# A scheduler's table of TensorE durations is replaced by traced ones, and its order offsets, holds and engine choices are newly drawn

## The chip, the cores and the metric

The kernel runs on 1 core of one Trainium2 chip. The metric is the device time of one execution in microseconds, the median of several runs. The engines have the profile's names: PE is TensorE (matmuls; PEld its weight loads), DVE is VectorE, ACT is ScalarE, POOL is GpSimd, SP is SyncE, which issues the transfers.

## The reference, cut to what matters

Two kinds of layer act on 256 tokens of width 1024, two layers of each. The first kind mixes with a sparse attention of three branches (compressed, selected, windowed) and a gated spatial product, then runs an FFN with a convolution over three tokens, then a gated embedding product (PLE). The second kind mixes with pooling, gated linear attention and latent attention, then runs a gated FFN. Everything is float32.

```python
def first_block(x, p, ...):
    for i in range(DEPTH):                       # 2
        z = rms_norm(h, pre_mix_g[i]) @ w_in[i]  # 1024 x 2328
        ...
        h = h + rms_norm(mix, post_mix_g[i])
        f = conv_ffn(rms_norm(h, pre_ffn_g[i]), w_up[i], conv_w[i], conv_b[i], w_down[i])
        h = h + rms_norm(f, post_ffn_g[i])
        gate = jax.nn.sigmoid(rms_norm(h, ple_norm_g[i]) @ w_ple_gate[i])
        h = h + gate * (p[i] @ w_ple_proj[i])

def conv_ffn(x, w_up, conv_w, conv_b, w_down):   # 1024 x 5632, 2816 x 1024
    ...
    g, up = jnp.split(hc, 2, axis=-1)
    return (jax.nn.silu(g) * up) @ w_down
```

The second kind has the same frame: a projection of 1024 x 5808, the mixers, an output projection, and an FFN with a gate and no convolution.

## The kernel before

**Tiling.** Tokens lie in two tiles of 128 (t = 0, 1). All large products are made from split operands: `split` (L965) loads a weight block of up to 128 x 1024 float32 into a buffer `raw`, casts it to float32r in `wh` (the high part) and subtracts that from the block into `wl` (the low part). Inputs are split in the same way: pairs of `x4` buffers (the instruction lists call them `x`) for the features, `ah` and `al` for the FFN's activations. A product then is three matmuls, high by high, high by low and low by high, added up in one PSUM bank. There are 7 buffers `raw`, 5 `wh` and 5 `wl`, and four PSUM pools of two banks: `pa`, `pb`, `upp` and `trp` (transposes).

**The FFN** (`ffn`, L1162) goes over 22 feature tiles of 128, two to a step. For each, `up_mm` multiplies two weight blocks by all 256 tokens into a bank of `upp` (48 matmuls of 256 columns); DVE multiplies the bank by the row scale (`z`, printed `u<-upp,u`), ACT and DVE do the convolution in the first kind of layer, ACT the silu, then a product `u<-u,u`, a cast into `ah` and a difference into `al`. `down_mm` (L1175) multiplies that by one block of the down weights into two banks of `pa` (t = 0) and two of `pb` (t = 1), 12 matmuls of 512 columns. The down products of the last four tiles are held back (`HELD`) and done first for t = 0, then for t = 1. `post_part` and `post_done` (L1090, L1101) then take the squares of the banks on ACT, two small operations on POOL, and update `h` (printed `c_h`) on DVE; the transposes of the new `h` on PE begin the next stage (`norm_fold`, L1070).

**What sets the order.** The program is first recorded, not emitted: each call on an engine makes an `Op` with its predecessors (`Recorder.add`, L202 and following). `schedule` (L364) then plays the operations through with a table of durations, `_cost` (L307): it always takes the engine that can start earliest and from its ready operations the one with the lowest `prio`, gives out buffers as they come free, and keeps the ports that DVE and POOL share apart (`_PORT`). `emit` (L517) writes the operations out in the resulting order; its call at L522 is therefore the line of nearly every instruction in the profile. Nothing of the plan is kept at run time but the order on each engine; the hardware waits on semaphores alone.

Three tables steer it, by phase (`m1` first mixer, `f1` first FFN and its middle and last steps `f1m` and `f1e`, `p1` PLE, `m2`, `f2`, `f2m`, `f2e` the same of the second kind, `s`, `c1`, `s2` set-up). `SHIFT` (L526) moves the `prio` of a group of operations (key: group and kind; kind 0 transfers, 1 weight splits, 2 the rest), `HOLD` (L645) adds to the time from which a group may start, and `ALT` (L703) lists operations that go to another engine (`_alternative`, L275): casts and copies between ACT and DVE, two-input operations and subtractions between DVE and POOL. A phase's entries hold for every layer that runs through it. The middle steps share one set, so that all of them have one pattern: seven in each layer for `f1m`.

Of the kernel before, what the change touches and what calls it, by code (L numbers as in the profile page):

```python
# [293 lines left out]
def _n(lz):  # L294
    return int(np.prod(lz.shape[1:]))
# [11 lines left out]
def _cost(eng, meth, args, kw, reads, writes):  # L307
# [6 lines left out]
    if eng == "tensor":  # L314
        if meth == "transpose":
            return 107.0, None
        rhs = args[2]
        c = _n(rhs)
        if rhs.dtype == F32:
            d = 2 * max(2 * c / 2.4, 107.0)  # L320
        elif rhs.dtype == F32R:
            d = c / 2.4 if c >= 256 else 4 * c / 2.4
        else:
            d = c / 2.4
        return d, None
# [191 lines left out]
def emit(nc, order):  # L517
    for op in order:
# [9 lines left out]
        (0, 0): 11, (0, 2): -701  # L528
    },
# [5 lines left out]
    },  # L535
# [5 lines left out]
    },  # L541
    "f1m": {
        (1, 0): -520, (1, 1): -3630, (1, 2): -723, (2, 0): -251, (2, 1): 188, (2, 2): -699
    },
# [11 lines left out]
    },  # L556
# [5 lines left out]
    },  # L562
    "f2m": {
        (1, 0): -676, (1, 1): -278, (1, 2): -631, (2, 1): -3, (2, 2): -666
    },
# [23 lines left out]
    },  # L589
# [1422 lines left out]
```

## Time and profile before

| | |
|---|---|
| median of 3 runs | 1585.4 us (1585.31 to 1591.89) |
| profiled execution, its span from first to last instruction | 1583.9 us |
| PE busy | 1562.3 us, 99% |
| PEld busy | 1358.9 us, 86% |
| DVE busy | 1083.7 us, 68% |
| ACT busy | 761.7 us, 48% |
| POOL busy | 492.3 us, 31% |
| read from HBM | 267.94 MB, 170 GB/s over the span |
| PE's share of the chain of waits | 96% |

The page gives no time of its own for the profiled execution but the span; the median of the runs is 1.5 us longer than it. The granted TensorE clock is 0.999 of full speed over the span. Matmuls are pipelined and their ends are modelled: two that follow each other at full rate overlap in the drawing, and the distance of their starts is what one of them costs. A wait that the profile lists is idle time in front of an instruction with the releaser that came last. An instruction list names buffers with numbers; in the profile's rows they are left out.

### The profile page before, as it was taken

To read this page: it belongs to the slowest core of one execution; us is meant where nothing else is said; L and a number is where in the kernel's file an instruction comes from. 1 tells how busy PE (TensorE), PEld (TensorE's weight loads), DVE (VectorE), ACT (ScalarE), POOL (GpSimd) and SP (SyncE) were. 2 spreads that over 40 slices of the span, in tenths; PEclk is the share of its full clock that TensorE was granted. 3 is DMA by queue.
4 is the path that set the end of the run, shared out by engine and by line. 5 is a ranking of instruction groups with operands and counts; after the bars stand their busy time and mean duration, and the time that the engine had idled before them with its cause. 6 is when DMAs were issued, how large, how long until landed. Compare 5 with 4: busy or idle time off the path is not lost.

```text
span 1583.9 us, 24617 instructions
## 1 busy us (share of the span) xinstructions
PE 1562.3 (99%) x9421; PEld 1358.9 (86%) x9421; DVE 1083.7 (68%) x1582; ACT 761.7 (48%) x1333; POOL 492.3 (31%) x428
## 2 busy tenths in 40 slices
PE   7999999999999999999999999999999999999998
PEld 6778999988778999988888888999988888889997
DVE  6777877888777877886645647566566455675664
ACT  4566555554666545556453444323354534343242
POOL 2433111122433111115233552323443326424233
PEclk9999999999999999999999999999999999999999
DMA  8643765745644656736534556566555344555571
GB/s 271 221 147 103 216 186 176 217 129 172 202 128 129 211 180 189 211 121 194 180 109 132 166 186 193 172 188 188 163 183 186 107 139 160 193 173 174 178 224 38
DMA packets 264091, 270.60 MB, mean 171 GB/s; under 512 B 11698, under 2 KB 196645, under 8 KB 263973
## 3 DMA queue, kind: packets, MB, share of 16 engines
q1 hardware_dynamic: 263972, 269.03, 55.0%
q8 instruction: 74, 1.21, 0.3%
q14 instruction: 45, 0.36, 0.1%
HBM read 267.94 MB, written 1.05 MB: 170 GB/s over the span
## 4 chain that ended last, share of the span: by engine, by line
PE 96%; DVE 2%; ACT 1%; DMA 1%; SPq 0%; issue 0%; POOL 0%; DVEq 0%; POOLq 0%; ACTq 0%
PE pa L522 36%; PE upp L522 35%; PE pb L522 19%; PE trp L522 5%; DMA raw<-in_w_in_dram 1%; DVE wl L522 1%; DVE u L522 1%; SPq L522 0%; ACT L522 0%; ACT u L522 0%; ACT junk L522 0%; DVE x L522 0%; DVE wh L522 0%; ACT x L522 0%; POOL sm L522 0%
## 5 line engine op out<-in xcount | busy, mean ns | idle before, releaser
L522 ACT CAST wh<-raw 128x1024 fp32r<-128x1024 f32 (+3 forms) x382 | 393.0, 1033 | 470.3 <-PE upp L522 234.1
L522 DVE TENSOR_TENSOR wl<-raw,wh 128x1024 fp32r<-128x1024 f32 (+3 forms) x402 | 500.5, 1257 | 119.2 <-ACT wh L522 114.5
L522 PE MATMUL upp<-x,wh 128*128 128x256 f32 x2560 | 479.3, 283 | 0.0
L522 PE MATMUL pa<-wh,x 128*128 128x512 f32 (+1 forms) x1280 | 425.9, 402 | 3.7 <-DVE x L522 2.0
L522 PEld LDWEIGHTS upp<-x,wh 128*128 128x128 f32 x2560 | 406.3, 191 | 6.2 <-ACT wh L522 0.3
L522 PE MATMUL upp<-x,wl 128*128 128x256 f32 x1280 | 361.3, 283 | 1.5 <-DVE wl L522 1.5
L522 POOL TENSOR_TENSOR wl<-raw,wh 128x1024 fp32r<-128x1024 f32 (+2 forms) x94 | 228.7, 2436 | 282.8 <-ACT wh L522 121.7
L522 PEld LDWEIGHTS pa<-wh,x 128*128 128x128 f32 x1280 | 236.7, 189 | 53.2 <-ACT u L522 2.6
L522 PE MATMUL pa<-wl,x 128*128 128x512 f32 (+1 forms) x640 | 251.9, 401 | 0.0
L522 PEld LDWEIGHTS upp<-x,wl 128*128 128x128 f32 x1280 | 244.6, 191 | 3.4 <-DVE wl L522 2.0
L522 POOL TENSOR_TENSOR u<-u,u 128x256 f32<-128x256 f32 (+4 forms) x98 | 109.3, 1117 | 328.0 <-ACT u L522 288.0
L522 DVE CAST wh<-raw 128x1024 fp32r<-128x1024 f32 (+3 forms) x114 | 89.3, 787 | 100.3 <-PE pa L522 38.7
L522 PE MATMUL pb<-wh,x 128*128 128x512 f32 (+2 forms) x496 | 157.4, 384 | 0.0
L522 PEld LDWEIGHTS pa<-wl,x 128*128 128x128 f32 x640 | 120.8, 189 | 21.4 <-DVE u L522 0.8
L522 DVE TENSOR_TENSOR u<-upp,u 128x512 f32<-128x512 f32 x80 | 55.2, 690 | 72.4 <-PE upp L522 71.6
L522 PEld LDWEIGHTS pb<-wh,x 128*128 128x128 f32 x496 | 90.4, 188 | 15.8 <-ACT wh L522 0.6
L522 PE MATMUL pb<-wl,x 128*128 128x512 f32 (+2 forms) x248 | 92.2, 381 | 0.0
L522 PE MATMUL trp<-c_ident,u 128*128 128x128 f32 (+4 forms) x415 | 79.5, 274 | 2.6 <-DMA u<-in_pre_mix_g_dram 1.9
L522 POOL TENSOR_TENSOR sm<-sm,c_nhalf 128x1 f32<-128x1 f32 (+1 forms) x60 | 47.9, 799 | 106.3 <-DVE sm L522 104.3
L522 DVE SCALAR_TENSOR_TENSOR u<-u,c_cols_conv_w,u 128x254 f32<-128x254 f32 (+1 forms) x176 | 73.5, 478 | 0.0
L522 ACT ACTIVATE u<-u 128x256 f32<-128x256 f32 (+1 forms) x100 | 44.5, 445 | 55.5 <-DVE u L522 49.6
L522 POOL TENSOR_TENSOR al<-u,ah 128x256 fp32r<-128x256 f32 x22 | 22.6, 1027 | 148.0 <-ACT ah L522 78.0
(209 smaller groups left out, 2092.3 us busy)
## 6 DMA issues: line engine op xcount, KB each, us to landing
raw<-in_w_in_dram SPq DMA_DIRECT2D x112, 512.0 KB, 4.0
raw<-in_w_up_dram SPq DMA_DIRECT2D x88, 512.0 KB, 4.2
raw<-in_w_ffn_gu_dram SPq DMA_DIRECT2D x88, 512.0 KB, 4.8
raw<-in_w_down_dram SPq DMA_DIRECT2D x44, 512.0 KB, 4.4
raw<-in_w_ffn_down_dram SPq DMA_DIRECT2D x44, 512.0 KB, 4.1
raw<-in_w_o_dram SPq DMA_DIRECT2D x32, 512.0 KB, 4.0
raw<-in_cmp_w_dram SPq DMA_DIRECT2D x16, 512.0 KB, 4.9
raw<-in_w_ple_gate_dram SPq DMA_DIRECT2D x16, 512.0 KB, 3.9
```

Of the source, the lines that this page charges most:

```text
L522: f(*args, **kw)
```

## The change

The duration table `_cost` gets new values for PE: a float32r matmul of 256 or more columns costs 10.8 ns more, a float32 matmul 2.5 ns more and, where it contracts over 64 rows or fewer, another 190; a transpose costs 106.5 instead of 107. `SHIFT`, `HOLD` and `ALT` are replaced throughout (some 900 numbers). Two comments are gone. Nothing else differs: the same operations are recorded with the same predecessors.

```diff
     if eng == "tensor":
         if meth == "transpose":
-            return 107.0, None
+            return 106.5, None
         rhs = args[2]
         c = _n(rhs)
         if rhs.dtype == F32:
-            d = 2 * max(2 * c / 2.4, 107.0)
+            d = 2 * max(2 * c / 2.4, 107.0) + 2.5
+            if rhs.shape[0] <= 64:
+                d += 190.0
         elif rhs.dtype == F32R:
-            d = c / 2.4 if c >= 256 else 4 * c / 2.4
+            d = c / 2.4 + 10.8 if c >= 256 else 4 * c / 2.4
         else:
             d = c / 2.4
         return d, None
...
 SHIFT = {
     "c1": {
-        (0, 0): 11, (0, 2): -701
+        (0, 0): 148, (0, 2): -137
     },
...
 ALT = {
...
     "f1m": {
-        62, 81, 142
+        66, 142, 143, 146, 147
     },
```

What this does to the lists is shown at three places.

**Place 1: DVE and POOL in the last middle steps of the second FFN (`f2`, `f2m`).** `raw` to `wh` is the cast, `raw,wh` to `wl` the subtraction. DVE and then POOL, before:

```order
L522 CAST wh3_68<-raw3_61 128x1024
L522 CAST wh0_65<-raw6_64 128x1024
L522 CAST wh4_69<-raw1_59 128x1024
L522 TENSOR_TENSOR wl3_73<-raw3_61,wh3_68 128x1024
L522 TENSOR_TENSOR wl4_74<-raw1_59,wh4_69 128x1024
L522 CAST wh2_67<-raw2_60 128x1024
```

```order
L522 TENSOR_TENSOR al1_117<-u22_106,ah1_112 128x256
L522 TENSOR_TENSOR wl1_71<-raw6_64,wh0_65 128x1024
L522 TENSOR_TENSOR u20_104<-u2_86,u5_89 128x256
L522 TENSOR_TENSOR wl4_74<-raw5_63,wh4_69 128x1024
L522 TENSOR_TENSOR al2_118<-u12_96,ah2_113 128x256
```

and with the change:

```order
L524 CAST wh2_67<-raw3_61 128x1024
L524 CAST wh4_69<-raw0_58 128x1024
L524 CAST wh3_68<-raw1_59 128x1024
L524 TENSOR_TENSOR u16_100<-upp0_227,u14_98 128x512
L524 TENSOR_TENSOR u0_84<-u24_108,u16_100 128x256
L524 TENSOR_TENSOR wl4_74<-raw2_60,wh1_66 128x1024
```

```order
L524 TENSOR_TENSOR u21_105<-u6_90,u8_92 128x256
L524 TENSOR_TENSOR wl3_73<-raw4_62,wh0_65 128x1024
L524 TENSOR_TENSOR wl1_71<-raw3_61,wh2_67 128x1024
L524 TENSOR_TENSOR al1_117<-u21_105,ah2_113 128x256
L524 TENSOR_TENSOR wl2_72<-raw0_58,wh4_69 128x1024
L524 TENSOR_TENSOR wl0_70<-raw1_59,wh3_68 128x1024
```

DVE's fifth row of before, the subtraction of the block that it had cast two rows earlier, is POOL's third row now (`wl1` from `raw3` and `wh2`), and so are the two subtractions after it; DVE keeps the three casts.

**Place 2: PE at the end of the first FFN, where the PLE begins.** `ah`, `al` are the held down products, `c_h` the transposes of the new `h`, and the last rows the first matmuls on the new `x`. Before:

```order
L522 MATMUL pb0_225<-wh4_69,ah1_112 128x512
L522 MATMUL pb1_226<-wh4_69,ah1_112 128x512
L522 MATMUL pb0_225<-wl1_71,ah1_112 128x512
L522 MATMUL trp0_229<-c_ident0_190,c_h0_191 128x128 x4
L522 MATMUL pb0_225<-wh4_69,al1_117 128x512
L522 MATMUL trp1_230<-c_ident0_190,c_h0_191 128x128 x4
L522 MATMUL pb1_226<-wl1_71,ah1_112 128x512
L522 MATMUL pb1_226<-wh4_69,al1_117 128x512
L522 MATMUL pa1_224<-wh0_65,x41_76 128x512
```

and with the change:

```order
L524 MATMUL pb0_225<-wh0_65,ah1_112 128x512
L524 MATMUL trp0_229<-c_ident0_190,c_h0_191 128x128 x4
L524 MATMUL pb0_225<-wl0_70,ah1_112 128x512
L524 MATMUL trp1_230<-c_ident0_190,c_h0_191 128x128 x4
L524 MATMUL pb0_225<-wh0_65,al1_117 128x512
L524 MATMUL pb1_226<-wh0_65,ah1_112 128x512
L524 MATMUL pb1_226<-wl0_70,ah1_112 128x512
L524 MATMUL pb1_226<-wh0_65,al1_117 128x512
L524 MATMUL pa0_223<-wh4_69,x40_75 128x512
```

Both groups of transposes stand two down matmuls earlier, so that five instead of three down matmuls lie between the first group and the first matmul on `x`. The six `pa` matmuls ahead of this stretch, whose banks `h` is made from, stand one place earlier than before.

**Place 3: POOL in the middle steps of the first FFN (`f1m`).** Two steps and a half, before:

```order
L522 TENSOR_TENSOR u19_103<-u0_84,u2_86 128x256
L522 TENSOR_TENSOR u5_89<-u13_97,u16_100 128x256
L522 TENSOR_TENSOR u20_104<-u11_95,u14_98 128x256
L522 TENSOR_TENSOR u9_93<-u3_87,u8_92 128x256
L522 TENSOR_TENSOR u7_91<-u15_99,u26_110 128x256
```

and with the change:

```order
L524 TENSOR_TENSOR u14_98<-u17_101,u1_85 128x256
L524 TENSOR_TENSOR wl4_74<-raw1_59,wh3_68 128x1024
L524 TENSOR_TENSOR u2_86<-u20_104,u25_109 128x256
L524 TENSOR_TENSOR wl0_70<-raw3_61,wh0_65 128x1024
L524 TENSOR_TENSOR u5_89<-u15_99,u11_95 128x256
```

POOL makes one product and one weight subtraction in each step now, where it made two products; DVE has the other product and, in place of the subtraction, a second weight cast and an activation cast that were ACT's.

## Rows read from the trace of the kernel before

**Rows 1.** The page, busy us (share of the span) and instructions, first line

```profile
PE 1562.3 (99%) x9421; PEld 1358.9 (86%) x9421; DVE 1083.7 (68%) x1582; ACT 761.7 (48%) x1333; POOL 492.3 (31%) x428
```

**Rows 2.** Timeline, first and last matmul: start us, us, engine, line, operation, out<-in

```profile
5.61 1.09 PE L522 MATMUL trp<-c_ident,c_h 128*128 128x128 f32 x4 [5.61 <-DMA c_h<-in_x_dram]
...
1577.07 0.39 PE L522 MATMUL pb<-wh,al 128*128 128x512 f32 x1
```

**Rows 3.** Waits of PE, the eight longest: us in total, times, longest us

```profile
PE trp L522 <- DMA c_h<-in_x_dram: 5.6, 1, 5.6
PE pa L522 <- DVE x L522: 2.0, 3, 0.8
PE trp L522 <- DMA u<-in_pre_mix_g_dram: 1.9, 1, 1.9
PE upp L522 <- DVE wl L522: 1.5, 2, 0.8
PE pa L522 <- ACT u L522: 1.3, 2, 0.6
PE trp L522 <- DVE x L522: 0.9, 1, 0.9
PE trp L522 <- DVE u L522: 0.5, 1, 0.5
PE upp L522 <- DVE x L522: 0.3, 2, 0.2
```

**Rows 4.** Timeline of PE near the end, two matmuls of 512 columns

```profile
1576.39 0.39 PE L522 MATMUL pb<-wh,al 128*128 128x512 f32 x1
...
1576.62 0.39 PE L522 MATMUL pb<-wh,ah 128*128 128x512 f32 x1
```

**Rows 5.** Timeline of POOL, DVE and PE, last f2 steps, both layers (last row the second)

```profile
1068.59 2.86 POOL L522 TENSOR_TENSOR wl<-raw,wh 128x1024 fp32r<-128x1024 f32 x1 [2.58 <-DVE wh L522]
...
1069.10 4.55 DVE L522 TENSOR_TENSOR wl<-raw,wh 128x1024 fp32r<-128x1024 f32 x2
...
1071.41 0.40 PE L522 MATMUL upp<-x,wh 128*128 128x256 f32 x2
1072.58 0.39 PE L522 MATMUL upp<-x,wl 128*128 128x256 f32 x1 [0.77 <-DVE wl L522]
...
1073.04 0.28 PE L522 MATMUL upp<-x,wl 128*128 128x256 f32 x1
1073.16 0.28 PE L522 MATMUL upp<-x,wh 128*128 128x256 f32 x1
...
1501.32 0.38 PE L522 MATMUL upp<-x,wl 128*128 128x256 f32 x1 [0.77 <-DVE wl L522]
```

**Rows 6.** Groups by form, 160 to 320 us: busy us, mean ns | idle before, releasers

```profile
L522 DVE TENSOR_TENSOR wl<-raw,wh 128x1024 fp32r<-128x1024 f32 x58 | 70.6, 1227 | 15.4 <-ACT wh L522 14.7
...
L522 DVE CAST wh<-raw 128x1024 fp32r<-128x1024 f32 x9 | 6.3, 695 | 9.1 <-PE pb L522 8.7 <-PE upp L522 0.4
...
L522 DVE TENSOR_TENSOR u<-u,u 128x256 f32<-128x256 f32 x2 | 0.8, 418 | 0.0
L522 DVE CAST ah<-u 128x256 fp32r<-128x256 f32 x2 | 0.6, 290 | 0.6 <-POOL u L522 0.6
...
L522 POOL TENSOR_TENSOR u<-u,u 128x256 f32<-128x256 f32 x17 | 19.5, 1146 | 121.5 <-ACT u L522 117.9 <-issue 3.5
```

**Rows 7.** Groups by form of POOL, 960 to 1120 us

```profile
L522 POOL TENSOR_TENSOR wl<-raw,wh 128x1024 fp32r<-128x1024 f32 x13 | 32.4, 2494 | 38.0 <-ACT wh L522 18.2 <-DVE wh L522 9.3 <-issue 7.2
```

**Rows 8.** Timeline at the seam from the first FFN to the PLE, first layer

```profile
339.33 1.42 DVE L522 SCALAR_TENSOR_TENSOR c_h<-u,sm,c_h 128x512 f32<-128x512 f32 x2 [0.36 <-POOL sm L522]
...
340.25 0.60 PE L522 MATMUL trp<-c_ident,c_h 128*128 128x128 f32 x4
...
342.73 0.47 PE L522 MATMUL pa<-wh,x 128*128 128x512 f32 x1 [0.75 <-DVE x L522]
```

**Rows 9.** One middle step, busy us (x) of PE, PEld, DVE, ACT, POOL; clock, DMA share, GB/s

```profile
204.51:221.57 17.06, 17.06 (x122) 16.01 (x122) 13.08 (x19) 8.66 (x13) 2.15 (x2) 1.00 0.62 184
```

More of the change, by code (lines that the diff above doesn't have):

```diff
@@ L527 @@
     "c1": {
-        (0, 0): 11, (0, 2): -701
+        (0, 0): 148, (0, 2): -137
     },
     "f1": {
[4 rows of a table removed]
[4 rows of a table added]
     },
     "f1e": {
[4 rows of a table removed]
[4 rows of a table added]
     },
     "f1m": {
-        (1, 0): -520, (1, 1): -3630, (1, 2): -723, (2, 0): -251, (2, 1): 188, (2, 2): -699
+        (1, 0): -1530, (1, 1): -914, (1, 2): -670, (2, 0): 5043, (2, 1): 1147, (2, 2): -717
     },
     "f2": {
[10 rows of a table removed]
[10 rows of a table added]
     },
     "f2e": {
[4 rows of a table removed]
[4 rows of a table added]
     },
     "f2m": {
-        (1, 0): -676, (1, 1): -278, (1, 2): -631, (2, 1): -3, (2, 2): -666
+        (1, 0): 3215, (1, 1): -118, (1, 2): 32, (2, 0): -366, (2, 1): -1515, (2, 2): -1484
     },
     "m1": {
[22 rows of a table removed]
[21 rows of a table added]
     },
     "m2": {
[39 rows of a table removed]
[38 rows of a table added]
     },
     "p1": {
[5 rows of a table removed]
[5 rows of a table added]
     },
     "s": {
-        (0, 0): 76, (0, 2): 156
+        (0, 0): 87
     },
     "s2": {
-        (0, 0): 185
+        (0, 0): -3032, (0, 2): 1944
     },
@@ L646 @@
     "c1": {
-        (0, 0): 974, (0, 2): 1486
+        (0, 2): 1903
     },
     "f1": {
-        (3, 1): 62, (5, 0): 106, (5, 2): 7, (6, 2): 1094, (9, 2): 18, (12, 2): 519, (14, 1): 1238
+        (0, 0): 89, (1, 0): 153, (3, 0): 723, (3, 1): 207, (3, 2): 5, (5, 0): 1696, (6, 0): 261, (6, 2): 782,
+        (12, 2): 4, (13, 0): 289
     },
     "f1e": {
-        (1, 0): 569, (1, 1): 203, (2, 1): 693, (3, 0): 782, (6, 0): 548, (10, 2): 7, (11, 2): 115, (12, 2): 256,
-        (14, 2): 270
-    },
-    "f1m": {
-        (1, 0): 1474, (1, 1): 252, (2, 1): 275
+        (2, 0): 182, (2, 1): 390, (4, 1): 477, (12, 2): 358
     },
     "f2": {
[4 rows of a table removed]
[4 rows of a table added]
     },
     "f2e": {
-        (1, 1): 953, (2, 1): 1454, (3, 1): 191, (4, 1): 75, (5, 1): 294
+        (6, 0): 841, (6, 1): 120
     },
     "f2m": {
-        (1, 0): 3995, (1, 1): 715, (2, 1): 268
+        (1, 1): 2200, (2, 0): 21
     },
     "m1": {
[8 rows of a table removed]
[7 rows of a table added]
     },
     "m2": {
[15 rows of a table removed]
[14 rows of a table added]
     },
     "p1": {
-        (3, 2): 15, (6, 2): 4, (8, 0): 580, (8, 1): 2246, (10, 0): 1337, (10, 1): 3584, (11, 2): 70, (12, 1):
-        386, (13, 0): 1023, (13, 2): 251, (15, 0): 2398, (15, 1): 1400, (18, 2): 643
+        (6, 2): 4, (7, 0): 976, (8, 1): 2446, (10, 1): 3650, (12, 1): 998, (12, 2): 354, (13, 2): 245, (14, 0):
+        667, (15, 0): 1949, (15, 1): 922, (18, 2): 639
+    },
+    "s2": {
+        (0, 2): 61
     },
@@ L703 @@
 ALT = {
+    "c1": {
+        10
+    },
     "f1": {
-        79, 137, 148, 149, 216, 217
+        42, 51, 57, 61, 76, 79, 137, 139, 149, 152, 216, 217, 218
     },
     "f1e": {
-        28, 62, 224, 302, 303, 306, 336, 371, 372, 439, 504
+        62, 81, 108, 143, 144, 146, 161, 162, 242, 303, 371, 439, 504
     },
     "f1m": {
-        62, 81, 142
+        66, 142, 143, 146, 147
     },
     "f2": {
-        17, 31, 32, 39, 53, 145, 167, 168, 170, 226, 228, 230, 238, 279, 307, 308, 311, 349, 350, 405, 424, 482,
-        483, 520, 575, 576, 580, 621, 622, 649, 654, 674, 747, 765, 792, 793, 821, 822, 824, 896, 940, 968, 969,
-        972, 973
[4 rows of a table added]
     },
     "f2e": {
-        56, 57, 76, 103, 132, 206, 278, 280, 286, 312, 340, 342, 374, 402, 403, 407
+        29, 56, 58, 75, 102, 103, 130, 132, 135, 204, 208, 223, 250, 251, 282, 285, 286, 312, 313, 340, 341,
+        342, 345, 347, 374
     },
     "f2m": {
-        1, 28, 57, 58, 76, 130, 131, 134
+        1, 2, 28, 29, 57, 58, 60, 61, 132
     },
     "m1": {
[4 rows of a table removed]
[4 rows of a table added]
     },
     "m2": {
[6 rows of a table removed]
[7 rows of a table added]
     },
     "p1": {
-        5, 16, 32, 35, 37
+        31, 35, 84, 142
     },
     "s": {
-        5, 6, 9, 11
+        9, 11, 27
     },
     "s2": {
-        7, 18, 19, 21, 27, 34, 35, 36, 43
+        17, 18, 33, 35, 43, 48
     },
```

251 rows, old and new, of tables (ALT, HOLD, SHIFT) are left out of this document.

## The prediction

> **What bounds the kernel now.** I read the busy table first. PE is busy for 1562.3 us of a span of 1583.9 [rows 1]; the other 21.6 us are the most that better order alone could show. The first and last matmul give two fixed pieces of it [rows 2]: nothing runs on PE before 5.61 us, and the last matmul starts at 1577.07 and is over 0.39 us later, 6.4 us before the end. That leaves 9.6 us of idle PE between 5.6 and 1577.5. Then PE's list of waits [rows 3]: the eight largest make 14.0 us; 5.6 is the lead-in, 1.9 the wait for the first gain vector at 8.6 us, and 6.5 us in eleven waits stand in the body. No engine, queue or transfer bounds the kernel but PE; DVE (68%), ACT (48%) and POOL (31%) only have to be in time.
>
> A busy PE hides a little more. Matmuls of 512 columns start 0.23 us apart while each is drawn 0.39 us long [rows 4], so a wait is shown about 0.16 us too short. Eleven of them hide 1.8 us. What order can win in the body is therefore 6.5 + 1.8 = **8.3 us**, 0.5% of the time.
>
> Durations come from the profiled execution. Its span is 1583.9; the median of the three runs is 1585.4, so I add 1.5 us to every sum.
>
> **The change, part by part.**
>
> *The PE table.* It enters the schedule alone. No duration in it is executed, so it costs nothing itself; what counts is the order that it yields, together with the new offsets and holds.
>
> *PE's work.* The order lists hold the same matmuls, in number and in shape, before and after (9063 rows of work on each side); nothing on PE is an engine choice. Cost 0. SP issues the same 583 transfers, its last four unchanged.
>
> *Head and tail.* Up to the first matmul on weights PE's rows are the same but for one transpose that no longer stands between two weight matmuls; the first transfers, up to the third block of w_in, are issued in the same order, and the end is the same chain (squares of the last pb banks on ACT, two small POOL operations, DVE, the store). Cost 0, hidden by nothing, but unchanged.
>
> *The last f2 steps (place 1).* Here the trace shows what a collision costs. Two weight subtractions of DVE took 4.55 us together while POOL ran one of its own for 2.86 [rows 5]; elsewhere one takes 70.6 / 58 = 1.22 on DVE [rows 6]. So DVE lost 4.55 - 2.44 = 2.1 us, and PE, whose two matmuls from 1071.41 on would have been followed 0.24 later, at 1071.65, went on at 1072.58: 0.93 lost, of which 0.77 is shown as a wait. The same stands at 1501.32 in the second layer. In the new order this subtraction is POOL's, behind DVE's cast of the same tile; between the last matmul on its weight buffer's old contents and the first that reads the difference PE has 27 matmuls of 256 columns and 17 of 512, at spacings of 0.12 and 0.23 us [rows 4, 5] 7.1 us. Against it stand a cast of 0.70, the POOL subtraction of 2.49 to 2.86 and one more of that length ahead of it [rows 5 to 7]: 6.4 us at worst. I take the wait as gone: 2 x 0.93 = **-1.9 us**. What is late next there is POOL, with four such subtractions near each other.
>
> *The seam from the first FFN to the PLE (place 2).* The first matmul on the new x waits 0.75 us for DVE [rows 8]. Between the first four transposes of h and that matmul PE has three matmuls and four transposes now and gets five and four: 2 x 0.23 = 0.45 us more cover. But the transposes themselves move up with the pa matmuls ahead of them by only one place, and they already start 0.2 us behind the half of c_h that they read (339.33 + 0.71, against 340.25) [rows 8]. So the second 0.23 turns into a wait in front of the transposes. I take one place: 0.23 in each of two layers, **-0.5 us**; the bounds are 0 and -0.9.
>
> *The middle steps of the first FFN (place 3).* There are 7 in each layer, 14 in all, each 17.06 us with PE busy throughout; DVE is busy for 13.08 and POOL for 2.2 [rows 9]. In each, DVE gives one weight subtraction to POOL (-1.22) and takes one weight cast (6.3 / 9 = +0.70), one product u (0.42) and the cast of an activation (0.6 / 2 = 0.30) [rows 6]: 13.3 us. POOL gives away a product (-1.15) and gets the subtraction (+2.49): 3.5 us. ACT is relieved of a weight cast and an activation cast. PE still needs 17.06, so the step costs **0**: the cover is DVE's 3.8 us of idle time in each. If that cover is gone, see the second rival. The weights that POOL makes there are those of the down product, and PE reads them 109 matmuls of 256 and 25 of 512 columns after their buffer comes free, 18.8 us.
>
> *Everything else.* Of the other engine choices (altogether 84 more weight casts and 40 fewer weight subtractions on DVE) the trace shows no row where PE ends up waiting for a longer time. The remaining waits of the body are 6.5 - 1.5 - 1.5 = 3.5 us in seven places, 4.6 with what they hide. All of them stand in mixer stages that are redrawn. Bounds: all gone, -4.6; as many new ones, +4.6. I take 0, since nearest to a redrawn order under the same rules is the order that the trace shows.
>
> Sum: 1583.9 - 1.9 - 0.5 = 1581.5 for the span, **1583.0 us** for the run.
>
> **A rule weighed against the trace.** The pair in [rows 5] shows DVE held for 2.1 of the 2.86 us that POOL's operation took, and POOL itself lengthened by 0.37 over its 2.49 [rows 5, 7]. The Trainium skill, "SBUF — State Buffer", section "Who interferes with whom", says that DVE and GpSimd arbitrate for one shared port pair and that the one that comes second "fully blocks"; by that rule moving a two-input operation from DVE to GpSimd buys nothing while the other is at work. By that rule a step's DVE is held for the whole 2.49, which makes 13.3 + 2.49 = 15.8 us of 17.06: the sum stays at 1583.0, unless what is held is what PE reads next. The trace bears the rule out as far as one pair can, and it speaks against place 3, where POOL had no weight subtraction until now; that case is the second rival.
>
> **The rivals.**
>
> *A, the waits of the body go.* For it: the old table planned a 256-column matmul at 109 ns, where the trace shows pairs 0.12 us apart [rows 5], so its plan and the run drift by a tenth in the FFNs, and the new one doesn't. Against it: DVE's and POOL's planned times are untouched, and a plan in which PE is too fast makes producers early, which is slack the new order loses. All 8.3 us gone gives 1583.9 - 8.3 + 1.5 = **1577.1 us**, 0.5% faster.
>
> *B, POOL holds DVE in the first FFN.* Each of the 14 middle steps now has a POOL subtraction of 2.49 us on a DVE that is busy for 13.3 of 17.06. One hold of 2.1 us fits into DVE's idle 3.8 as long as no operation that PE needs soon is behind it. It decides from the point where the held operation is the subtraction that PE reads next, as at 1069.10, or where the multiply that frees the upp bank queues behind it. Then each step loses what the f2 seam lost: 14 x 0.93 = 13.0 us, so 1583.0 + 13.0 = **1596.0 us**, 0.7% slower. For it: that exact row. Against it: the weights that POOL makes are due 18 us later, so POOL may be the one that waits. A whole 2.49 in each step would be 34.9 us and 1617.9.
>
> *C, the change does nothing to the time.* Every wait that goes comes back elsewhere: 1585.4. This is inside "within 0.5%", as is the forecast.
>
> **How the numbers follow.** 0.5% is 7.9 us, about what a measurement of this kernel can tell from no change; faster means below 1577.5 and slower above 1593.3. The forecast with C, and all between them: 0.53. A, or A with part of the start's 1.9 us as well: 0.27. B and like collisions in the mixers of the second block, where POOL has most of its subtractions: 0.20. The range reaches down to A with that 1.9 us and a little of the loading phase, 1574, and up to B and one further us, 1597; about one in ten lies beyond either end. The part that the likeliest case alone would take is 1579 to 1588.
>
> **What would show it.** In the profile after: PE's busy time still 1560 to 1564 and its first and last matmul where they are; no wait of "upp" for DVE's wl of 0.7 us near 1072 and 1501; the wait of pa for DVE x behind the FFN seam down to about 0.5; middle steps of 17.06 us with DVE near 13.3, POOL near 3.5. Steps of 18 us, or DVE subtractions of more than 3 us beside POOL's between 180 and 300 us, would be B. The forecast is wrong if PE's waits in the body sum to under 2 us or to over 12.

## The result and the profile after

| | before | with the change |
|---|---|---|
| median | 1585.4 us | 1600.1 us (1597.5 to 1601.8, 4 runs) |
| ratio to the kernel before, 95% interval | | 1.0084 [1.0065, 1.0103] |
| profiled execution, span | 1583.9 us | 1595.7 us |

The change made the kernel slower by 0.8%, and its median lies just above the range of the prediction (1574 to 1597); 1583.0 was forecast. The profiled execution is the shortest of the four, so the profile accounts for 11.8 us of the 14.7 between the medians.

The busy table, first line, answers to [rows 1]:

```profile
PE 1569.6 (98%) x9421; PEld 1364.5 (86%) x9421; DVE 1200.8 (75%) x1641; ACT 659.6 (41%) x1216; POOL 634.6 (40%) x486
```

DVE is busy for 117 us more and POOL for 142 more, ACT for 102 less. 84 casts of 0.7 us less 40 subtractions of 1.2 would give DVE some 10 us, so most of DVE's growth is operations that got longer. PE's waits, the longest (us in total, times, longest), answer to [rows 3]:

```profile
PE trp L524 <- DMA c_h<-in_x_dram: 5.6, 1, 5.6
PE trp L524 <- DVE c_h L524: 3.9, 2, 1.9
PE trp L524 <- DMA u<-in_mlp_out_g_dram: 3.9, 1, 3.9
PE pb L524 <- DVE wh L524: 2.6, 2, 1.3
PE trp L524 <- DMA u<-in_pre_mix_g_dram: 1.5, 1, 1.5
PE pa L524 <- POOL x L524: 0.6, 1, 0.6
PE pa L524 <- ACT x L524: 0.5, 2, 0.3
```

Three of these lines are new: 3.9 us for c_h and 2.6 us for a cast wh, each once in both layers of the second kind, and 3.9 us for a tile of gain vectors at the start. Gone are the 1.5 us for DVE's wl and the 2.0 us for DVE's x of [rows 3]. The timeline at the first of the new places, the end of the second kind's mixer (DVE, POOL and PE; start us, us, engine, operation):

```profile
958.59 3.58 DVE L524 SCALAR_TENSOR_TENSOR c_h<-u,sm,c_h 128x512 f32<-128x512 f32 x2 [0.39 <-POOL sm L524]
...
959.26 2.36 POOL L524 TENSOR_TENSOR wl<-raw,wh 128x1024 fp32r<-128x1024 f32 x1 [0.71 <-ACT wh L524]
...
959.40 0.66 PE L524 MATMUL trp<-c_ident,c_h 128*128 128x128 f32 x4
...
962.22 0.66 PE L524 MATMUL trp<-c_ident,c_h 128*128 128x128 f32 x4 [1.94 <-DVE c_h L524]
```

The second half by itself:

```profile
959.26 2.91 DVE L524 SCALAR_TENSOR_TENSOR c_h<-u,sm,c_h 128x512 f32<-128x512 f32 x1
```

The two halves of c_h take 3.58 us together; the same pair takes 1.42 in [rows 8]. POOL's weight subtraction and the second half both start at 959.26 in the trace, and the rows can't tell which came first; but POOL's operation takes 2.36 and ends at 961.62, and the second half takes 2.91 and ends at 962.17. PE's transposes of that half start 2.2 us later than PE's own pace would have it. 38 us earlier stands the other one:

```profile
920.75 2.38 POOL L524 TENSOR_TENSOR wl<-raw,wh 128x1024 fp32r<-128x1024 f32 x1
920.81 0.69 DVE L524 TENSOR_TENSOR u<-pb,sm 128x512 f32<-128x512 f32 x1 [1.25 <-POOL sm L524]
...
921.42 2.25 DVE L524 CAST wh<-raw 128x1024 fp32r<-128x1024 f32 x1
...
923.73 0.50 PE L524 MATMUL pb<-wh,x 128*128 128x512 f32 x1 [1.27 <-DVE wh L524]
```

Beside this POOL operation DVE's product that reads a PSUM bank (pb) takes its usual 0.69; the cast behind it, from SBUF to SBUF, takes 2.25 instead of 0.69. That cast was ACT's before the change. Both places come again 432 us later. By the distances of matmul starts the four cost 2 x (2.19 + 1.43) = 7.2 us.

At the start SP issues the last gain vector at 19.28 us (before: 15.84), and PE stops for it:

```profile
19.28 0.29 SPq L524 DMA_DIRECT2D u<-in_mlp_out_g_dram  x1
```

```profile
22.61 0.41 PE L524 MATMUL trp<-c_ident,u 104*128 104x104 f32 x1 [3.87 <-DMA u<-in_mlp_out_g_dram]
```

Behind two of the stops the clock is lower as well (stretches; PE, PEld, DVE, ACT, POOL busy us; clock, DMA share, GB/s):

```profile
22.61:28.70 6.09, 6.08 (x15) 4.83 (x16) 3.82 (x4) 4.04 (x4) 0.00 (x0) 0.51 0.96 327
...
962.22:966.20 3.98, 3.98 (x20) 3.34 (x21) 3.83 (x7) 3.18 (x6) 0.06 (x1) 1.00 0.42 132
...
1393.76:1397.60 3.84, 3.84 (x12) 3.22 (x13) 3.31 (x5) 2.45 (x5) 0.00 (x0) 0.56 0.43 137
```

Behind the 3.9 us in which PE stood still, and behind the second of the two c_h waits, the granted clock is near its lower level of 1.2 GHz over stretches of 6.1 and 3.8 us; a 512-column matmul then starts 0.43 us after the one before instead of 0.23. By the distances of the 512-column matmuls that is 2.8 us more at the start and 1.4 behind 1393.76. Behind the first c_h wait it stays at 2.4 GHz.

In all, the first 50 us go like this, before and with the change:

```profile
0.00:50.00 50.00, 41.63 (x211) 34.47 (x212) 36.08 (x68) 22.07 (x32) 11.10 (x18) 1.00 0.90 286
```

```profile
0.00:50.00 50.00, 38.08 (x184) 31.45 (x185) 31.14 (x52) 22.52 (x33) 14.87 (x22) 0.93 0.81 253
```

PE starts 184 matmuls in them instead of 211.

The middle steps of the first FFN answer to [rows 9]:

```profile
232.80:249.98 17.18, 17.18 (x122) 16.04 (x121) 14.30 (x21) 7.01 (x12) 4.28 (x3) 1.00 0.62 183
```

### The profile page after: what moved, and what is told of

The parts are those of the page before. It is cut to its first block, busy times and chain, and to the rows that moved or that the text cites. A ratio compares the mean times of both kernels' runs of the same rounds, so it can differ in the third digit from the quotient of the medians.

```text
span 1595.7 us, 24664 instructions
## 1 busy us (share of the span) xinstructions
PE 1569.6 (98%) x9421; PEld 1364.5 (86%) x9421; DVE 1200.8 (75%) x1641; ACT 659.6 (41%) x1216; POOL 634.6 (40%) x486
## 4 chain that ended last, share of the span: by engine, by line
PE 95%; DVE 1%; DMA 1%; ACT 1%; POOL 1%; issue 0%; SPq 0%; DVEq 0%; POOLq 0%; ACTq 0%
PE upp L524 35%; PE pa L524 35%; PE pb L524 19%; PE trp L524 5%; DVE c_h L524 1%; DMA raw<-in_cmp_w_dram 0%; POOL sm L524 0%; DVE u L524 0%; DVE wh L524 0%; ACT junk L524 0%; SPq L524 0%; DMA c_h<-in_x_dram 0%; POOL wl L524 0%; DMA u<-in_mlp_out_g_dram 0%; ACT x L524 0%
## 5 line engine op out<-in xcount | busy, mean ns | idle before, releaser
L524 DVE TENSOR_TENSOR wl<-raw,wh 128x1024 fp32r<-128x1024 f32 (+2 forms) x358 | 475.8, 1340 | 64.3 <-ACT wh L524 61.6
L524 ACT CAST wh<-raw 128x1024 fp32r<-128x1024 f32 (+4 forms) x306 | 310.0, 1021 | 415.7 <-PE upp L524 181.7
L524 POOL TENSOR_TENSOR wl<-raw,wh 128x1024 fp32r<-128x1024 f32 (+2 forms) x138 | 344.9, 2506 | 229.8 <-DVE wh L524 97.4
L524 PE MATMUL pa<-wh,x 128*128 128x512 f32 (+1 forms) x1280 | 433.0, 404 | 1.1 <-POOL x L524 0.6
L524 PE MATMUL upp<-x,wl 128*128 128x256 f32 x1280 | 354.1, 283 | 0.0
L524 DVE CAST wh<-raw 128x1024 fp32r<-128x1024 f32 (+2 forms) x190 | 187.0, 988 | 127.8 <-PE pa L524 46.0
L524 DVE SCALAR_TENSOR_TENSOR u<-u,c_cols_conv_w,u 128x255 f32<-128x255 f32 (+1 forms) x176 | 74.8, 475 | 6.9 <-ACT u L524 6.7
L524 POOL TENSOR_SCALAR sm<-sm 128x1 f32<-128x1 f32 (+2 forms) x40 | 16.8, 421 | 147.8 <-ACT junk L524 117.6
L524 ACT ACTIVATE u<-pa,sm 128x512 f32<-128x512 f32 (+2 forms) x62 | 41.4, 676 | 73.4 <-PE pa L524 73.4
L524 POOL TENSOR_TENSOR al<-u,ah 128x256 fp32r<-128x256 f32 x38 | 38.1, 1005 | 82.6 <-DVE ah L524 77.5
```

Of the source, the lines that this page charges most:

```text
L524: f(*args, **kw)
```

## The experiments

Every kernel was timed in five rounds beside the kernel before. Nine of the twelve hold one kind of edit: a POOL operation on one column makes a subtraction of POOL wait for a DVE operation. It is put into the finished list, so that no order on any engine changes:

```diff
+def _behind(order, late, early, mark):
+    for a, b in zip(_nth(order, late, "gpsimd"), _nth(order, early, "vector")):
+        src = b.args[0].bitcast(F32)
+        ...
+        tok.eng, tok.meth, tok.args, tok.kw = "gpsimd", "tensor_scalar", (mark, src, 1.0, None), {"op0": ALU.mult}
+        order.insert(order.index(a), tok)
```

**1. POOL behind DVE at the two places**, the second half of c_h and the cast.

```diff
+    _behind(order, ("f2", 39), ("m2", 1605), mark)
+    _behind(order, ("m2", 1424), ("m2", 1454), mark)
```

> The changed kernel with four small POOL operations more: ahead of the weight subtractions that start at 920.75 and 959.26 us (and at their twins in the second layer, 432 us later) POOL copies one column of the result of DVE's cast of 921.42 or of the second half of c_h, so that the subtraction starts behind DVE's operation instead of just ahead of it. All engine orders are otherwise the same. Port theory (POOL's subtraction holds DVE for its whole length, and PE waits for what DVE makes): PE's gaps of 2.2 us at 962 and 1394 and of 1.4 us at 924 and 1355 go, 7.2 us, and with them the nine matmuls at half clock behind 1394, 1.8 us: about 1591, the two halves of c_h together 1.4 us in both layers, the cast 0.7. Rival (PE is simply ahead of its operands there: the weights that POOL makes, or the transposes, come late anyhow): DVE's operations get short, but PE waits as long one operation later: 1599 to 1601.

1589.2 us, ratio 1.0014 [1.0003, 1.0025]: 10.9 us come back between the medians. The two profiled executions differ by 8.2 us (1595.7 and 1587.5), which is about what the four places and the clock behind one of them cost; the other 2.7 us of the medians no kept trace accounts for. The timeline at the c_h place (mark is the small operation), the second half of c_h by itself, and the cast:

```profile
957.06 1.41 DVE L549 SCALAR_TENSOR_TENSOR c_h<-u,sm,c_h 128x512 f32<-128x512 f32 x2 [0.39 <-POOL sm L549]
...
958.56 0.24 POOL L549 TENSOR_SCALAR mark<-c_h 128x1 f32<-128x1 f32 x1 [1.54 <-DVE c_h L549]
...
958.75 2.41 POOL L549 TENSOR_TENSOR wl<-raw,wh 128x1024 fp32r<-128x1024 f32 x1
```

```profile
957.73 0.75 DVE L549 SCALAR_TENSOR_TENSOR c_h<-u,sm,c_h 128x512 f32<-128x512 f32 x1
```

```profile
921.43 0.69 DVE L549 CAST wh<-raw 128x1024 fp32r<-128x1024 f32 x1
```

The pair takes 1.41, its second half 0.75 instead of 2.91, the cast 0.69, all four waits are gone, and no new one stands behind them. POOL's two subtractions start some 1 and 2 us later than they could, and PE's list has no wait for them. The rival falls. The wait for the gains stays, at 2.9 us.

**2. The gain transpose later, and both edits.** PE's transpose of the gains and its copy are set 18 matmuls later.

```diff
+    tr = _nth(order, ("s", 26), "tensor")[0]
+    _later(order, [tr] + _nth(order, ("s", 27), "vector"), pe[pe.index(tr) + 18])
```

> The changed kernel with one transpose of PE (of the tile of small gain vectors, which waits 3.87 us for its transfer at 22.61 us) and its copy on DVE set 18 matmuls later; nothing else moves. Theory (one transfer that the plan has early and that SP issues late stops PE, which has other work ready): the gap of 4.0 us goes and so do the thirteen matmuls at half clock behind it, 2.7 us: about 1593.4. Rival (the start is bound by the weight transfers: what PE would do next isn't there either): PE waits for a wh, wl or x instead, 1597 to 1600.

> Both edits of the two runs before this together. Theory: the gains add up, 1600.1 - 9.0 - 6.7 = 1584.4, level with the kernel before. Rival (waits that go come back elsewhere): above 1592.

1598.0 and 1589.9 us, ratios 1.0066 [1.0049, 1.0083] and 1.0013 [1.0003, 1.0023]. The intervals with and without the edit overlap, for the changed kernel and for that of experiment 1. The theory falls: the wait for the gains is gone, but PE stops at 27.96 us for the next thing (PE's waits, this edit alone):

```profile
PE pa L549 <- ACT wh L549: 2.8, 1, 2.8
```

That wh comes from a weight block that SP had issued behind the gains. What was open: which order at the start sets the time.

**3. One half of the change each.** The scheduler's PE durations put back under the new tables, and the new durations put under the old tables (the lines of `_cost` in the diff of the change, reversed or alone).

```diff
-            d = c / 2.4 + 10.8 if c >= 256 else 4 * c / 2.4
+            d = c / 2.4 if c >= 256 else 4 * c / 2.4
```

> The changed kernel with the durations of PE in the scheduler's table as they were before; offsets, holds and engine choices stay the new ones. Theory (single collisions of a newly drawn order, POOL's subtractions ahead of DVE's operations, cost the time; the table of durations moves them but doesn't remove them): the order is drawn again, collisions stand at other places, 1590 to 1612. Rival (the new durations make the plan run late against the chip, and that is what costs): near the kernel before, 1583 to 1589.

> The kernel before with the new durations of PE in the scheduler's table alone; offsets, holds and engine choices stay the old ones. Theory (the tables of offsets and holds fit only the durations that they were drawn with, so either half of the change alone spoils the order): clearly slower than both, 1620 to 1720. Rival (truer durations give a better or equal order by themselves): 1578 to 1590.

1702.4 and 1654.1 us, ratios 1.0728 [1.0707, 1.0748] and 1.0422 [1.0403, 1.0441]. The first was expected at 1590 to 1612 and is far worse; the second came as expected. Durations and tables belong together: with either half alone PE's waits are many and everywhere (the longest of the first kernel's):

```profile
PE trp L522 <- DVE c_h L522: 8.6, 5, 3.8
PE trp L522 <- DVE u L522: 6.6, 5, 3.4
PE upp L522 <- DVE wl L522: 6.1, 6, 2.1
```

So the 0.8% can't be divided between the durations and the tables; "the new durations cost it" and "the tables cost it" are both the wrong question.

**4. The same edit in the kernel before.** First POOL's subtraction of [rows 5] behind DVE's first one (the first line), then also a place in the first kind of layer.

```diff
+    _behind(order, ("f2", 973), ("f2", 941), mark)
+    _behind(order, ("m1", 188), ("m1", 360), mark)
```

> The kernel before with one small POOL operation more in each layer of the second kind: the weight subtraction of POOL at 1068.59 us waits for DVE's subtraction of 1069.10, as the plan has it. Theory (that is the 0.93 us that PE loses at 1072.58 and at 1501.32): both waits go, 1.9 us, 1584.6 where the kernel before has 1586.5. Rival (PE waits for the same weights anyhow, or for POOL's one operation later): no difference, and a wait of 0.7 us or more stays within 5 us of the place.

> The kernel before with the small POOL operation at 1068.59 us that took it to 1583.5, and a second such one in the first kind of layer: the weight subtraction of POOL at 382.71 us waits for DVE's small products that it held for 2.1 us, and behind which PE waited for x at 389.49. Theory (the same hold, one more place): that gap of 1.1 us goes in the second of the two layers, 1582.4. Rival (x is late for other reasons, or POOL's subtraction gets late): 1583.5 or a little more, with a wait near 389 that stays.

1583.5 us, ratio 0.9982 [0.9973, 0.9991], and 1582.5 us, ratio 0.9981 [0.9972, 0.9989]: the only kernels of the study that beat the one before. The pair of DVE that took 4.55 us in [rows 5], and the second place, before and with the edit:

```profile
1069.03 2.35 DVE L547 TENSOR_TENSOR wl<-raw,wh 128x1024 fp32r<-128x1024 f32 x2
```

```profile
382.71 3.32 POOL L522 TENSOR_TENSOR wl<-raw,wh 128x1024 fp32r<-128x1024 f32 x1 [4.82 <-DVE wh L522]
...
383.68 2.56 DVE L522 TENSOR_TENSOR u<-u,c_rope_tok 128x32 f32<-128x32 f32 x3
...
389.49 0.33 PE L522 MATMUL trp<-wh,x 128*60 128x256 f32 x1 [0.94 <-DVE x L522]
```

```profile
385.32 0.35 DVE L547 TENSOR_TENSOR u<-u,c_rope_tok 128x32 f32<-128x32 f32 x3
...
385.97 2.41 POOL L547 TENSOR_TENSOR wl<-raw,wh 128x1024 fp32r<-128x1024 f32 x1
...
390.02 0.28 PE L547 MATMUL trp<-wh,x 128*60 128x256 f32 x1
```

Three tiny products took 2.56 us beside POOL and 0.35 ahead of it, and PE's wait six us later is gone. That the second edit shortens the time isn't shown: the intervals of the two ratios overlap almost wholly, and the profiled executions have spans of 1581.8 and 1582.2 us; the second has 3.4 us at half clock from 105.4 us on, which the first has not.

**5. POOL behind DVE wherever the plan has it there.** Each long two-input operation of POOL that the plan starts within 0.3 us of the end of a DVE operation that it counts as using the shared port now waits for that operation.

```diff
+    for a in [x for x in order if x.eng == "gpsimd" and x.port == "pool_read" and x.dur > 800]:
+        e = [x for x in order if x.eng == "vector" and x.port in ("two", "wide") and x.start < a.start - 1e-6]
+        if not e or a.start - e[-1].end > 300.0 or e[-1].args[0].dtype not in (F32, F32R):
+            continue
```

> The changed kernel with 133 small POOL operations more: wherever the plan starts a long two-input operation of POOL within 0.3 us of the end of a DVE operation that uses the shared port, POOL now waits for that DVE operation. The time that DVE is held falls from 170 us to under 60. Theory (a hold costs only where PE reads next what DVE makes, which four of them did): as with the first four, 1588 to 1591. Rival (170 us of held DVE delays PE all over, in small gaps too): under 1584. If POOL's 133 operations make POOL late, above 1593.

1607.4 us, ratio 1.0126 [1.0111, 1.0141]: the third of the outcomes. DVE was held less, but by far less than expected (142 us; 163 with the four edits of experiment 1, 170 in the changed kernel, 62 in the kernel before: the sum, over DVE's operations beside one of POOL, of what each took beyond the fifth percentile of its form, where that is over 0.15 us). The likely reason is that the next DVE operation meets the delayed subtraction; it was not followed place by place. And now PE waits for POOL:

```profile
PE upp L549 <- POOL wl L549: 6.4, 8, 1.2
```

These eight waits are a third of the 18.5 us between the profiled executions of experiment 1 and of this one (1587.5 and 1606.0); the rest is not taken apart. Fewer holds did not make a faster kernel. In the changed kernel there are some 155 held operations, and four of them stand in front of PE's waits for DVE, 7.2 us.

**6. The start, three more orders.** All have the edit of experiment 1. The first has that of experiment 2 too, and two weight blocks ahead of others on SP's queue; the second puts two blocks (one of them issued among the gains) and two small weights behind the gains again, with the two blocks that PE needs next ahead of these; the third moves ACT's and DVE's operations on these blocks along.

```diff
+    blocks = [_nth(order, ("m1", k), "sync")[0] for k in (81, 128, 171, 277, 278, 145)]
+    _later(order, blocks, _nth(order, ("s", 25), "sync")[0])
+    _later(order, [_nth(order, ("m1", 129), "scalar")[0]], _nth(order, ("m1", 82), "scalar")[0])
+    _later(order, [_nth(order, ("m1", 146), "scalar")[0]], _nth(order, ("m1", 161), "scalar")[0])
+    _later(order, [_nth(order, ("m1", 130), "vector")[0]], _nth(order, ("m1", 83), "vector")[0])
```

The first two lines alone are the second kernel.

> The kernel with both edits, and on SP's queue two weight blocks of w_in that PE needs from 27 us on (they were issued at 19.6 to 20.5 us) set ahead of two blocks that it needs later. Theory (the order of the weight transfers sets the start, the late gain vectors only hid it): the 2.3 and 1.0 us that PE waits at 27 to 29 us for ACT's wh and DVE's wl go, and most of the matmuls at half clock behind them: the excess of the first 50 us falls from 10.6 to about 5.5 and the time from 1589.9 to about 1585. Rival (too few bytes have landed by then, whatever their order): PE waits as long for the next block, 1588 to 1591.

> The changed kernel with the four POOL operations that let its subtractions wait, and SP's queue alone changed at the start: one block of w_in and two small compression weights, which stood ahead of the constants and gain vectors (issued at 5.6 to 7.3 us), go behind them, and the two blocks that PE needs from 27 us on come first behind the gain vectors. PE's order is the changed kernel's own. Theory (each 512 KB block ahead of the constants and gain vectors brings them in some 1.4 us later, and PE, DVE and the blocks behind wait in turn; the kernel before had a block and two small weights fewer there): the gap of 3 to 4 us at 22.6 falls under 1 and the excess of the first 50 us from 11 to about 7: 1585. Rival (what PE does in the first 50 us in the new order needs more bytes early, in any order of transfers): a wait of the same size at another block, 1588 to 1591.

> As the run before with SP's queue changed at the start, and ACT's casts and DVE's subtraction of these blocks moved with them: ACT's queue took the block first that now lands last, so that its cast at 25.83 us waited 8.3 us and PE's block stood behind it. Now ACT casts the block that PE needs first, then the next, and the late one two places later. Theory (the start loses time because the order of SP, ACT and PE no longer fit to each other in time; blocks earlier in all three queues give it back): the wait of 5.2 us at 28.8 falls under 1.5, the excess of the first 50 us from 14 to 7 or 8, 1585 to 1586. Rival (what PE does in the first 50 us of the new order can't be fed faster): again a wait of 3 to 5 us at a later block, 1588 to 1592.

1591.2, 1591.5 and 1591.6 us; ratios 1.0025 [1.0014, 1.0036], 1.0033 [1.002, 1.0045] and 1.0031 [1.002, 1.0042]. Each time the expected wait went and one of 4.7 to 6.2 us came at another place, as the rivals said. The places tell why. In the second, ACT's queue still took first the block that now landed last. In the third (and, at 35.69 us, in the first) ACT stood in front of a tiny cast. The second kernel, then the third:

```profile
25.83 3.88 ACT L549 CAST wh<-raw 128x1024 fp32r<-128x1024 f32 x4 [8.31 <-DMA raw<-in_w_in_dram]
...
28.82 0.80 PE L549 MATMUL pa<-wh,x 128*128 128x512 f32 x1 [5.22 <-ACT wh L549]
```

```profile
35.00 0.19 ACT L549 CAST c_pf<-c_pi 128x2 f32<-128x2 int32 x1 [6.21 <-DMA c_pi<-in_positions_dram]
35.10 0.68 ACT L549 ACTIVATE u<-pa,sm 128x512 f32<-128x512 f32 x1
...
35.84 0.90 PE L549 MATMUL trp<-c_ident,u 128*128 128x128 f32 x3 [6.19 <-ACT u L549]
```

Behind the cast in ACT's queue is the read-out of a bank (`u<-pa,sm`) that PE's transposes need. In the kernel before this cast is DVE's, at 48.75 us, one of the choices that `ALT` changed. In the changed kernel itself it stands on ACT but waits for nothing:

```profile
34.73 0.19 ACT L524 CAST c_pf<-c_pi 128x2 f32<-128x2 int32 x1
```

So it is no part of that kernel's loss; it is what the start meets next once the stops ahead of it are gone.

**7. That cast 12 places later on ACT,** on top of the third kernel of experiment 6.

```diff
+    _later(order, [_nth(order, ("s2", 17), "scalar")[0]], _nth(order, ("m1", 473), "scalar")[0])
```

> As the run before, and one tiny cast of ACT (of the token positions, 128x2; the change's engine choices took it from DVE, at 48.7 us in the kernel before, to ACT, at 34.7 us) set 12 places later in ACT's queue. In the run before it waited 6.2 us for its transfer, with the read-out of a pa bank behind it that PE needed. Theory (a cast of 0.2 us that nobody needs for 50 us holds ACT's queue on a late transfer): the wait of 6.2 us at 35.8 goes, the excess of the first 50 us falls from 14 to 6 or 7, level with the kernel before, and the time to 1584 to 1586. Rival (the start can't be fed): a wait of 3 to 6 us again, 1588 to 1592.

1585.9 us, ratio 0.9999 [0.999, 1.0007]: level with the kernel before, so the start could be fed. The first 50 us:

```profile
0.00:50.00 50.00, 40.17 (x211) 32.64 (x211) 33.80 (x55) 25.02 (x38) 17.31 (x23) 1.00 0.87 284
```

The cast now runs at 49.77 us, and PE's list holds no wait over 0.7 us behind that for the first gain vector. With ten operations moved and four added, in a program of some 24,700 instructions, the whole loss is back. Which of the ten are needed was not tried: the move of the cast has no run without the moves of the blocks.

## Why the prediction was wrong

**The forecast let no hold reach PE; the cause stood among its rivals, at another place and price.** Rival B, "POOL holds DVE", is the larger part of what happened, but the prediction priced it where `f1m` gives POOL a new subtraction, and mentioned the second block's mixers only in passing. That its 1596.0 lies near the measured time is luck: it was counted from the 14 middle steps, and those grew by 0.12 us each where they were measured, not by 0.93. In the mixers of the second kind, just ahead of the FFN, the holds cost 7.2 us at four places, and another 1.4 us in the clock behind one of them. Experiment 1 shows it: with POOL held back at these places alone, all four waits go and the profiled execution is 8.2 us shorter.

**What adds up to the loss.** By the distances of matmul starts, against the median of the same form in the kernel before, the first 50 us cost 4.7 us more, the four places 7.2, the clock behind one of them 1.4. That is 13.3 us; the two profiled executions differ by 11.8, so all the rest together is some 1.5 us shorter than before.

**Failed step: "Everything else."** It bounded the rest by what PE waited for in the old order, 4.6 us either way, and took 0. The four places alone cost 8.6 us with the clock. The old order's waits are no bound for a new order's. What a better bound would have counted are the POOL subtractions that stand close to a DVE operation that PE reads next: there are 40 more subtractions on POOL and 84 more casts on DVE (the cast at 921.42 is one), and [rows 5] had the price of a hold, 2.1 us. Two misses in a layer of the second kind were enough.

**Failed step: "Head and tail."** Head and tail were called unchanged, since PE's rows and SP's transfers agree up to the third block. The first and last matmul did stay (5.62 us, and 6.4 before the end). But the stretch from there to 50 us has no term of its own in the sum. In it the change moved a block and two small weights on SP ahead of the gains, and the start lost 4.7 us: what the distances of matmul starts exceed their usual ones by grew from 6.9 to 11.6 in the first 50 us, 2.8 of it at half clock behind the stop for the gains. Experiment 7 shows that no transfer rate forces this: with another order on SP, ACT and DVE the excess is 8.1 (it stays 1.2 above the kernel before, and the shorter body makes up for that). That the order of the queues against the landing of transfers sets the start is what the places of the waits in experiments 2 and 6 say; for ACT's queue experiment 7 shows it, where one move gives 5.7 us over the kernel without it.

**f2 seam: right.** -1.9 forecast; no wait for wl is left there, and taking it out of the kernel before alone gave 2.9 us [1.4, 4.3] (experiment 4, from the ratio).

**PLE seam: right, a little small.** -0.5 forecast, bounds 0 and -0.9. In front of the first matmul on x PE's gap fell from 0.91 in each layer to 0.42 and 0.38, -1.0 together; the transposes ahead of it start 0.13 late in each layer now, so some -0.8 is left. Part of the cover did turn into a wait in front of the transposes, as the prediction said.

```profile
347.81 0.49 PE L524 MATMUL pa<-wh,x 128*128 128x512 f32 x1 [0.25 <-ACT x L524]
```

**f1 middle steps: almost.** No step lost 0.93, and POOL is the one with time. DVE is busy for 14.30 instead of the 13.3 that was worked out, 1.0 us of it held (its subtraction at 233.36 takes 2.35 beside POOL's of 232.23); the cover of 3.8 us took that, as the prediction said. The step grew to 17.18 all the same, 0.12 us more; were it so in all 14, 1.7 us. The lost time stands at one matmul: ACT's cast ah ends at 238.65 us, PE's weight load for it starts at 238.71, at the matmul instead of ahead of it, and the next matmul starts 0.35 us later instead of 0.23.

**Rival A** (the waits of the body go) came half true: of the 6.5 us of [rows 3] the changed kernel keeps 1.6 in PE's list, but the four new waits put 6.5 in their place, and its price of 1577.1 was not met. Whether the truer durations did that isn't shown: experiment 3's second kernel has them under tables drawn with the old ones, and that pair doesn't fit.

**The signs.** PE's busy time was to stay at 1560 to 1564 and is 1569.6; matmuls at half clock count as busy longer, and so this sign spoke. The other, waits of the body over 12 us, hardly did: PE's list has 8.1 there, 12.0 with the wait for the gains. A list of waits doesn't show the matmuls that run at half clock.

**Why the plan did not see it.** `schedule` keeps the shared port apart by the times of its plan, and `HOLD` delays some of POOL's subtractions there. Nothing of that reaches the chip: POOL starts when its operands are there. In the plan the subtraction of 959.26 us begins when the second half of c_h is through; on the chip its operand, ACT's wh, is ready at 959.18, and the second half is held. That the marks, which make the planned order real at the four places, bring the time back is shown; that truer durations of POOL's small operations would have sufficed was not tried.

**The rule.** The Trainium skill, "SBUF — State Buffer", section "Who interferes with whom", says that issue order and not the shape of the operations decides who blocks, and that a DVE operation with at most one SBUF input outside the two-port modes doesn't contend. The traces agree where they can tell: POOL's subtraction of 920.75 started 0.67 us ahead of DVE's cast, and the cast was held; in experiment 1 the cast and c_h's second half come first and take 0.69 and 0.75; and the product that reads pb took 0.69 beside POOL. The cast has a single input too, in SBUF, and yet was held; whether it ran in one of the excepted modes no run here shows.

## What to carry to other kernels

Where two engines share a port, a plan that only orders each engine by itself leaves their mutual order to chance: look for each long POOL operation whose start is not tied to the DVE operation that PE needs next, and tie those few (here a one-column read was enough), not all. A step that a prediction calls unchanged has to be followed on every queue up to the point where the queues are full; a cast of 0.2 us that waits for a late transfer holds its engine, and what PE needs from it, for as long as the transfer takes (6.2 us here). And constants of a plan that were drawn together are to be judged together.

## What was not expected of the hardware

Behind the same gap of 2.2 us the clock stayed at 2.4 GHz at 962 us and was near 1.2 GHz at 1394; why the one and not the other stays open. A one-column operation of POOL took 0.24 us at 958.56 (experiment 1) and 1.14 beside a subtraction of DVE; in experiment 5 such operations took 0.20 to 1.27 us. The one of 1.14, from experiment 4's first kernel:

```profile
1070.35 1.14 POOL L547 TENSOR_SCALAR mark<-wl 128x1 f32<-128x1 f32 x1 [4.41 <-DVE wl L547]
```
